# A transformer-style block on one core: first tile in halves, gain row by matmuls, sinks and mask steps later, last product by column halves

## The chip, the cores and the metric

The kernel runs on one core of a Trainium2 chip. Its time is the device time of one execution in microseconds (us); the figure for a kernel is the median of its runs. The names of the engines are those of the profile: PE is TensorE (matmuls and transposes; PEld are its weight loads), DVE is VectorE, ACT is ScalarE, POOL is GpSimd, SP is SyncE, which here only starts transfers.

## The reference, cut to what matters

The block works on 1024 tokens of 1024 channels. `rmsnorm` divides by the root of the mean square and multiplies by a gain per channel.

```python
h = rmsnorm(x, norm_g)                                 # per token: x * rsqrt(mean(x*x) + 1e-6) * norm_g
q, k, v, za, u, vs, zs, gm = split(h @ w_in)           # one combined projection
a = window_sink_attention(rope(q), rope(k), v, sinks)  # 16 heads, 2 key heads, window of chunks, a sink per head
a = (a * silu(za)) @ w_att_out
vs = layernorm(gelu(vs), sg_ln_g, sg_ln_b)
w = where(chunk-causal mask, sg_w, 0)                  # 8 groups of 128x128, over positions of a block of 128
sgo = ((gelu(u) * (w @ vs + sg_b)) * silu(zs)) @ w_sg_out
ga, gs = split(sigmoid(gm + b_merge))
x = x + (ga * a + gs * sgo) @ w_o
out = rmsnorm(x, final_g)
```

## The kernel before

**Tiles and number format.** Tokens and channels are cut into eight tiles of 128. The weights lie packed as 82 tiles of 128x1024 in DRAM. Every product is made of three matmuls on operands that are split into a high part (a cast, on ACT, L154) and a low part (what the cast left out, on DVE, L155): high by high, high by low, low by high. Most projections go through `gemm_pair`, which makes a 2x2 block of products with seven products instead of eight, from sums of the weight tiles and sums of the activations (`b11`, `t1`, `t2`, `b21`, `t3`, `b22`, `t4`). `product` (matmuls of L364) issues one of the seven: four slices of the contraction by three matmuls, 12 in all, each 128x128 by 128x512.

**Order of the work.** A scheduler orders most stages on each engine from the data dependences and the order of the source, so the order in the source is not that of an engine's queue; `after(a, b)` puts instruction a behind b. The attention stage has an order of its own, written out. Transfers are started by the queue of SP, some by POOL's and a few by ACT's; they leave a queue in the order in which it holds them.

**The start.** Thirteen matmuls without use for the result (`keep_busy`, L543) run on PE while the first data come. SP's queue starts the load of token tile 0 (512 KB), the broadcast of the row `norm_g` to all 128 partitions (4 KB read for each partition, 512 KB written), two weight tiles of the vs projection, token tile 1, and so on. For each token tile `scale_of` squares and sums a row on ACT (L571), `rstd_of` turns the sum into the factor in six steps (L132 on DVE, the root on ACT at L134, then four on DVE, the last at L144: a reciprocal and one Newton step), and `normed_tile` scales by the factor and the gain row on DVE in two halves (L585), transposes on PE (L591), casts the high part on ACT (L594), takes the low part on DVE (L595) and keeps a plain copy on ACT. `split_vs` splits the weight tiles; the low part of the first one is POOL's work (L621), that of the others DVE's. `vs_gemm(t)` makes, for one token tile, half of the vs channels: eight slices by three matmuls (L605) into one accumulator. The second half follows for all eight token tiles at once in eight accumulators.

**The two steps that move.** The sinks (16 numbers, spread over 128 partitions) are loaded on SP's queue with the last loads of this stage, and DVE turns their sign (L736, `nsink_sb`); the result is used in the attention stage. The mixing weights of the gating stage are loaded behind them, and DVE sets the masked quarter of each to zero (L757). They are used in the gating stage, which makes four calls of `gemm_pair`; in each, a DVE addition at L406 is the last to set `term[0]`.

**The end.** Four pairs of token tiles go through the last projection in the order of `T_ORDER`. In the last pair (p = 3) four products remain at the end: `by_b22`, `by_t3`, `by_b21`, and then `t4`, which completes the first half of the channels of row 1 (the second token tile of the pair). `add_and_square` adds the residual to a product (DVE, L1715) and squares and sums it on ACT (L1717). The factor for row 0 and row 1 comes from `rstd_of` with the first half's sum as its base. `scale_and_store` scales by factor and gain on DVE (L1737), or, where POOL has multiplied by the gain ahead of time (`scaled`), by the factor alone on ACT, and stores four pieces of 128x512, three started by SP and the last by ACT (L1735):

```python
        product(acc, ready[n, 6], ob["t4"], False)
        add_and_square(1, 0, acc, 1.0)
        scale_and_store(0)
        scale_and_store(1)
```

## Time and profile before

| | us |
|---|---|
| median of 3 runs | 929.79 (929.11, 929.79, 932.47) |
| profiled execution | 928.11 |
| span of its trace | 926.3 (granted clock 0.999 of full) |

By stretch of the span (busy us):

| stretch | what runs | PE | DVE | ACT | POOL |
|---|---|---|---|---|---|
| 0 to 30 | first tiles, first vs products | 23.96 | 19.03 | 20.67 | 3.24 |
| 30 to 160 | vs, its gelu, start of gating | 129.87 | 90.40 | 64.23 | 23.60 |
| 160 to 300 | gating, queries and keys | 140.00 | 95.06 | 57.63 | 27.88 |
| 300 to 560 | attention among others | 258.33 | 204.59 | 192.51 | 43.55 |
| 560 to 760 | branch outputs | 197.61 | 146.47 | 108.59 | 21.56 |
| 760 to 905 | branch outputs, last projection | 143.68 | 123.15 | 80.43 | 16.22 |
| 905 to 926 | last products, norm, stores | 13.93 | 12.98 | 6.75 | 5.06 |

The profile is of one execution, whose own time stands in the first table. A row of the instructions in order of time reads: start in us from the span's start, duration, engine, line of the kernel and operation, output<-inputs by the program's names, shapes, and in brackets how long the engine stood idle just before and what released it. A row of a stretch reads: stretch, its length, busy time and number of instructions of each engine, granted TensorE clock (1.00 is full), mean busy share of the 16 DMA engines, and GB/s. Busy times of PE are of matmuls that overlap in a pipeline, and their ends are modelled.

### The profile page before, as it was taken

The numbers are of one execution on the slowest core, as the hardware profiler recorded it, in microseconds if no ns is written. First come the engines' busy times: TensorE is split into PE (matmuls) and PEld (weight loads), VectorE is DVE, ScalarE is ACT, GpSimd is POOL, SyncE is SP. The second block draws the span as 40 slices with busy tenths as digits, with TensorE's granted clock in tenths as the row PEclk, the third lists the DMA queues.
The fourth block names the chain that finished last, engine by engine and source line by source line (L and its number), as shares of the span: only waits on it lengthen the run. The fifth ranks groups of instructions, "written<-read, shape, count | busy, mean of one in ns | idle before, by whom it ended". The sixth has DMA issues, their size and how long they took to land.

```text
span 926.3 us, 13136 instructions
## 1 busy us (share of the span) xinstructions
PE 907.4 (98%) x4285; PEld 749.9 (81%) x4285; DVE 691.7 (75%) x1234; ACT 530.8 (57%) x1054; POOL 141.1 (15%) x209
## 2 busy tenths in 40 slices
PE   7999999999999999999999999999999999999996
PEld 5788888888888888888888887888887887888885
DVE  6784776556678767777887778766598789579996
ACT  6973433334444556877778777434475475467443
POOL 1002222213011001321211110011100111210012
PEclk9999999999999999999999999999999999999999
DMA  7237788877778989999999994775568564998633
GB/s 261 92 114 218 178 146 185 175 189 219 239 267 259 283 266 308 203 266 271 260 343 246 241 269 138 278 257 187 174 207 319 176 205 151 297 314 286 206 112 116
DMA packets 128588, 206.62 MB, mean 223 GB/s; under 512 B 12584, under 2 KB 59176, under 8 KB 128520
## 3 DMA queue, kind: packets, MB, share of 16 engines
q1 hardware_dynamic: 107000, 146.79, 50.0%
q0 software_dynamic: 21376, 58.73, 26.3%
q8 instruction: 34, 0.56, 0.3%
q14 instruction: 34, 0.28, 0.1%
q10 hardware_dynamic: 144, 0.26, 0.1%
HBM read 148.98 MB, written 90.31 MB: 258 GB/s over the span
## 4 chain that ended last, share of the span: by engine, by line
PE 34%; DVE 14%; ACT 7%; issue 4%; DMA 3%; SPq 0%; ACTq 0%; DVEq 0%
PE ps_mm L364 17%; PE ps_o L364 10%; PE ps_tp L364 2%; ACT pr L1171 2%; PE ps_sc L364 2%; DVE sm L1161 2%; DVE pTb L1243 1%; DVE aT L1274 1%; ACT pr L1194 1%; DVE wl L155 1%; DVE bq L184 1%; PE ps_o L1260 1%; PE ps_sc L1136 1%; ACT aT L1273 1%; DMA s<-sums 1%
## 5 line engine op out<-in xcount | busy, mean ns | idle before, releaser
L154 ACT CAST wh<-s 128x1024 fp32r<-128x1024 f32 (+1 forms) x78 | 78.0, 1002 | 81.7 <-PE ps_mm L364 39.8
L155 DVE TENSOR_TENSOR wl<-s,wh 128x1024 fp32r<-128x1024 f32 (+1 forms) x78 | 91.6, 1174 | 20.9 <-ACT wh L154 20.7
L155 DVE TENSOR_TENSOR wl<-wr,wh 128x1024 fp32r<-128x1024 f32 (+1 forms) x64 | 60.3, 945 | 56.7 <-ACT wh L154 56.2
L154 ACT CAST wh<-wr 128x1024 fp32r<-128x1024 f32 (+1 forms) x64 | 53.0, 829 | 77.6 <-PE ps_mm L364 37.7
L310 POOL DMA_DIRECT2D sums<-in_w_dram x48 | 37.2, 936 | 212.3 <-PE ps_mm L605 63.2
L1171 ACT ACTIVATE pr<-ps_sc,sm 128x192 f32<-128x192 f32 (+2 forms) x128 | 51.2, 407 | 30.6 <-DVE sm L1162 22.0
L364 PE MATMUL ps_o<-T_b22h,wh 128*128 128x512 f32 x148 | 59.4, 401 | 0.0
L364 PE MATMUL ps_o<-T_t1h,wh 128*128 128x512 f32 x148 | 58.6, 396 | 0.3 <-ACT wh L154 0.2
L364 PE MATMUL ps_o<-T_t1h,wl 128*128 128x512 f32 x148 | 57.8, 391 | 0.2 <-DVE wl L155 0.2
L364 PE MATMUL ps_o<-T_b22l,wh 128*128 128x512 f32 x148 | 57.8, 391 | 0.0
L364 PE MATMUL ps_o<-T_b22h,wl 128*128 128x512 f32 x148 | 57.8, 390 | 0.0
L364 PE MATMUL ps_o<-T_t1l,wh 128*128 128x512 f32 x148 | 57.7, 390 | 0.0
L364 PE MATMUL ps_mm<-T_b11h,wl 128*128 128x512 f32 x140 | 54.8, 392 | 2.0 <-DVE wl L155 2.0
L364 PE MATMUL ps_mm<-T_t2h,wh 128*128 128x512 f32 x140 | 55.5, 396 | 0.0
L364 PE MATMUL ps_mm<-T_t4h,wh 128*128 128x512 f32 x140 | 55.0, 393 | 0.3 <-DVE x L402 0.3
L364 PE MATMUL ps_mm<-T_b11h,wh 128*128 128x512 f32 x140 | 55.1, 394 | 0.0
L364 PE MATMUL ps_mm<-T_t3h,wh 128*128 128x512 f32 x140 | 54.8, 391 | 0.0
L364 PE MATMUL ps_mm<-T_b11l,wh 128*128 128x512 f32 x140 | 54.7, 391 | 0.0
L364 PE MATMUL ps_mm<-T_t3h,wl 128*128 128x512 f32 x140 | 54.6, 390 | 0.0
L364 PE MATMUL ps_mm<-T_t4h,wl 128*128 128x512 f32 x140 | 54.6, 390 | 0.0
L364 PE MATMUL ps_mm<-T_t2h,wl 128*128 128x512 f32 x140 | 54.6, 390 | 0.0
L364 PE MATMUL ps_mm<-T_t4l,wh 128*128 128x512 f32 x140 | 54.5, 390 | 0.0
(370 smaller groups left out, 2469.0 us busy)
## 6 DMA issues: line engine op xcount, KB each, us to landing
wr<-in_w_dram SPq DMA_DIRECT2D x80, 256.0 KB
sums<-in_w_dram POOLq DMA_DIRECT2D x24, 512.0 KB, 6.5
s<-sums SPq DMA_DIRECT2D x24, 512.0 KB
wr<-in_w_dram SPq DMA_DIRECT2D x16, 512.0 KB
q_hl<-qhl SPq DMA_DIRECT2D x16, 512.0 KB
q<-q_hl SPq DMA_DIRECT2D x64, 128.0 KB
y_dr<-x POOLq DMA_DIRECT2D x28, 256.0 KB, 6.6
sums<-in_w_dram POOLq DMA_DIRECT2D x24, 256.0 KB, 7.9
```

Source lines behind the costliest of these rows:

```text
L154: nc.scalar.copy(hi, src)
L155: return nc.vector.tensor_sub(lo, src, hi.bitcast(F32))
L184: op(dst[:, i : i + 2, :], a[:, i : i + 2, :], c[:, i : i + 2, :])
L310: return lambda: paced(nc.gpsimd.dma_start(dst, src, accum_op=op))
L364: nc.tensor.matmul(acc, lt, rt, start=fresh and k == 0 and n == 0, stop=k == 3 and n == 2, skip_group_check=True,)
L1136: nc.tensor.matmul(sc[:, i, lo:hi], q_of[:, c, i * P : (i + 1) * P], kt[:, f, lo:hi], start=f == 0, stop=f == 1,)
L1161: nc.vector.tensor_reduce(st.nmax[:, c, :], st.sc[c][:, :, lo:hi], axis=mybir.AxisListType.X, op=ALU.min)
L1171: nc.scalar.activation(st.pr[:, i, place_of(c, lo, hi)], st.sc[c][:, i, lo:hi], AF.Exp, bias=st.nmax[:, c, i : i + 1], scale=-1.0, accum_o ...
L1194: nc.scalar.mul(v, v, st.inv[:, c, i : i + 1])
L1243: nc.vector.tensor_sub(st.b[lo, cols(c)], st.ends[hi, 0:256], st.b[hi, cols(c)].bitcast(F32))
L1260: nc.tensor.matmul(st.po[:, cs], lt, rt, start=i == 0, stop=i == len(terms) - 1, skip_group_check=True)
L1273: nc.scalar.copy(dst, out_of(there))
```

## The change

Start: the load of token tile 0 is two transfers of 256 KB. The gain row is loaded once (4 KB, started by ACT's queue) and spread to the partitions by two matmuls with a row of ones, one for each half, into two PSUM banks, from which `normed_tile` reads it. Four dummy matmuls stand ahead of them and one behind, in another bank, instead of 13. `rstd_of` adds the base within ACT's root and folds the last multiplication into the step before; the eight-column case has a function of its own with the old steps. The square of token tile 0 is taken in two halves, the first half's sum becoming the base of the factor. The first weight tile is split in two halves, on ACT and POOL. In `vs_gemm(0)` the first two slices are ordered by part: two high by high, two high by low, two low by high. The sign of the sinks is turned behind the last addition of the gating stage; the zeroing of the mixing weights stands behind the last low part of x. The transfers of both keep their place on SP's queue.

End: the last product is made in two halves of 256 columns of 12 matmuls each (`last_by_halves`), each followed by its own addition and square; the first half's sum becomes the base of the factor. Row 1's remaining pieces are scaled and stored in quarters: two on DVE, started by SP, two on ACT, started by ACT. Row 0's two stores are both started by SP.

```diff
@@ -97,6 +97,8 @@
+    g_row = mtile([P, D], F32, "wh", 3)[0:1, :]
+    nc.scalar.dma_start(g_row, norm_g.unsqueeze(0))
     plain = mtile([P, D], F32, "wl", 3)[:, 0:HALF]
@@ -126,20 +128,29 @@
-    def rstd_of(ss, scale, base=EPS, n=1):
-        ve = mtile([P, n], F32, f"st{n}", 16 if n == 1 else 5)
-        nc.vector.tensor_scalar(ve[:], ss, scale, base, op0=ALU.mult, op1=ALU.add)
-        rt = mtile([P, n], F32, f"st{n}", 16 if n == 1 else 5)
+    def stat():
+        return mtile([P, 1], F32, "st1", 16)
+    def rstd_of(ss, scale, base=None):
+        rt, r0, v, r = (stat() for _ in range(4))
+        nc.scalar.activation(rt[:], ss, AF.Sqrt, bias=eps_sb[:] if base is None else base[0], scale=scale)
+        nc.vector.tensor_scalar(
+            v[:], ss, -0.5 * scale, -0.5 * EPS if base is None else base[1], op0=ALU.mult, op1=ALU.add
+        )
+        nc.vector.reciprocal(r0[:], rt[:])
+        nc.vector.scalar_tensor_tensor(v[:], v[:], r0[:], r0[:], op0=ALU.mult, op1=ALU.mult)
+        nc.vector.tensor_scalar(r[:], v[:], 1.5, r0[:], op0=ALU.add, op1=ALU.mult)
+        return r
+    def rstd_of_tiles(var):
+        ve, rt, r0, e = (mtile([P, NT], F32, f"st{NT}", 5) for _ in range(4))
+        nc.vector.tensor_scalar(ve[:], var, 1.0, EPS, op0=ALU.mult, op1=ALU.add)
         nc.scalar.activation(rt[:], ve[:], AF.Sqrt)
-        r0 = mtile([P, n], F32, f"st{n}", 16 if n == 1 else 5)
         nc.vector.reciprocal(r0[:], rt[:])
-        e = mtile([P, n], F32, f"st{n}", 16 if n == 1 else 5)
-        if n == 1:
-            nc.vector.scalar_tensor_tensor(e[:], ve[:], r0[:], r0[:], op0=ALU.mult, op1=ALU.mult)
-        else:
-            nc.vector.tensor_mul(e[:], ve[:], r0[:])
-            nc.vector.tensor_mul(e[:], e[:], r0[:])
+        nc.vector.tensor_mul(e[:], ve[:], r0[:])
+        nc.vector.tensor_mul(e[:], e[:], r0[:])
         nc.vector.tensor_scalar(e[:], e[:], -0.5, 1.5, op0=ALU.mult, op1=ALU.add)
@@ -351,9 +362,9 @@
-    def product(acc, part, form, fresh, middle=lambda: None):
+    def product(acc, part, form, fresh, middle=lambda: None, cols=slice(0, HALF)):
         wh, wl = part
-        bh, bl = form
+        bh, bl = (v[:, :, cols] for v in form)
         for k in range(4):
@@ -525,15 +536,15 @@
-    def load_x(t):
+    def load_x(t, parts=1):
         xt = raw_tile()
-        nc.sync.dma_start(xt[:], x[t * P : (t + 1) * P, :])
+        for c in range(parts):
+            cs = slice(c * D // parts, (c + 1) * D // parts)
+            nc.sync.dma_start(xt[:, cs], x[t * P : (t + 1) * P, cs])
         return xt
-    x_in = {0: load_x(0)}
-    g_in = mtile([P, D], F32, "wh", 3)
+    x_in = {0: load_x(0, 2)}
     junk = mtile([P, D], F32, "wl", 3)
-    nc.sync.dma_start(g_in[:], norm_g.partition_broadcast(P))
@@ -542,8 +553,12 @@
-    idle = bank("sc")
-    keep_busy(13)
+    idle = bank("o")
+    keep_busy(4)
+    g_in = [bank("sc") for _ in range(2)]
+    for j in range(2):
+        nc.tensor.matmul(g_in[j][:], plain[0:1, 0:P], g_row[:, half_of(j)], start=True, stop=True)
+    keep_busy(1)
@@ -563,11 +578,18 @@
-    casts = []
+    casts, los = [], []
         xt = x_in[t] if t in x_in else load_x(t)
-        ss = mtile([P, 1], F32, "st1", 16)
+        if t == 0:
+            s0, s1, base, half_base = (stat() for _ in range(4))
+            for c, ss in enumerate((s0, s1)):
+                nc.scalar.activation(junk[:, half_of(c)], xt[:, half_of(c)], AF.Square, accum_out=ss[:])
+            nc.vector.tensor_scalar(base[:], s0[:], 1.0 / D, EPS, op0=ALU.mult, op1=ALU.add)
+            nc.vector.tensor_scalar_mul(half_base[:], base[:], -0.5)
+            return xt, rstd_of(s1[:], 1.0 / D, (base[:], half_base[:]))
+        ss = stat()
         square = nc.scalar.activation(junk[:], xt[:], AF.Square, accum_out=ss[:])
@@ -583,7 +605,7 @@
             nc.vector.scalar_tensor_tensor(
-                xt[:, cs], xt[:, cs], r[:], g_in[:, cs], op0=ALU.mult, op1=ALU.mult
+                xt[:, cs], xt[:, cs], r[:], g_in[j][:], op0=ALU.mult, op1=ALU.mult
             )
@@ -592,7 +614,7 @@
             casts.append(nc.scalar.copy(hi, p3))
-            nc.vector.tensor_sub(lo, p3, hi.bitcast(F32))
+            los.append(nc.vector.tensor_sub(lo, p3, hi.bitcast(F32)))
             turned.append((f[f"f{j + 1}{t // 4 + 1}"][:, :, tokens(t)], p3))
@@ -617,13 +639,23 @@
         else:
-            nc.scalar.copy(hi, raw)
-            nc.gpsimd.tensor_tensor(lo, raw, hi.bitcast(F32), op=ALU.subtract)
+            for k in range(2):
+                nc.scalar.copy(hi[:, k, :], raw[:, k, :])
+                nc.gpsimd.tensor_tensor(lo[:, k, :], raw[:, k, :], hi[:, k, :].bitcast(F32), op=ALU.subtract)
         vs_w.extend((hi[:, k, :], lo[:, k, :]) for k in range(2))
         acc = bank("mm")
-        for k in range(KC):
+        if t == 0:
+            by_part = [[], [], []]
+            for k in range(2):
+                hi, lo = (v[:, k, :] for v in quarter_of(t, 0))
+                wh, wl = vs_w[k]
+                for part, pair in zip(by_part, ((hi, wh), (hi, wl), (lo, wh))):
+                    part.append(pair)
+            for n, (lt, rt) in enumerate(by_part[0] + by_part[1] + by_part[2]):
+                nc.tensor.matmul(acc[:], lt, rt, start=n == 0, stop=False)
+        for k in range(2 if t == 0 else 0, KC):
             vs_step(acc[:], t, k, *vs_w[k])
@@ -733,7 +765,6 @@
         )
-    nc.vector.tensor_scalar_mul(nsink_sb[:], sink_sb[:], -1.0)
     nc.sync.dma_start(bm_sb[:], b_merge)
@@ -754,7 +785,7 @@
     nc.sync.dma_start(mix_w[:], sg_w)
-    nc.vector.memset(mix_w[64:128, :, 0:64], 0.0)
+    after(nc.vector.memset(mix_w[64:128, :, 0:64], 0.0), los[-1])
     ones = mtile([P, P], F32, "ones", 1, pool)
@@ -763,7 +794,7 @@
     def normalize():
-        r = rstd_of(mv[:, :, 1], 1.0, n=NT)
+        r = rstd_of_tiles(mv[:, :, 1])
         for t in range(NT):
@@ -832,6 +863,7 @@
     stage.close()
+    after(nc.vector.tensor_scalar_mul(nsink_sb[:], sink_sb[:], -1.0), term[0])
@@ -1713,16 +1745,46 @@
             pace[0] = (nc.vector.tensor_sub if sign < 0 else nc.vector.tensor_add)(z, z, src)
-            ss = mtile([P, 1], F32, "st1", 16)
+            ss = stat()
             nc.scalar.activation(bank("tp")[:], z, AF.Square, accum_out=ss[:])
             if i in sq:
-                sq[i] = rstd_of(ss[:], 1.0 / D, sq[i][:])
+                sq[i] = rstd_of(ss[:], 1.0 / D, sq[i])
             else:
-                nc.vector.tensor_scalar(ss[:], ss[:], 1.0 / D, EPS, op0=ALU.mult, op1=ALU.add)
-                sq[i] = ss
+                sq[i] = based(ss, EPS)
+        def based(ss, base):
+            b, minus = stat(), stat()
+            nc.vector.tensor_scalar(b[:], ss[:], 1.0 / D, base, op0=ALU.mult, op1=ALU.add)
+            nc.vector.tensor_scalar_mul(minus[:], b[:], -0.5)
+            return b[:], minus[:]
+        def last_by_halves():
+            for c in range(2):
+                cs = slice(c * 256, (c + 1) * 256)
+                z = xr[:, 2, cs]
+                product(acc[:, cs], ready[n, 6], ob["t4"], False, cols=cs)
+                pace[0] = nc.vector.tensor_add(z, z, acc[:, cs])
+                ss = stat()
+                nc.scalar.activation(bank("tp")[:, cs], z, AF.Square, accum_out=ss[:])
+                if c == 0:
+                    sq[1] = based(ss, sq[1][0])
+                else:
+                    sq[1] = rstd_of(ss[:], 1.0 / D, sq[1])
+            r = sq[1]
+            row = slice((t + 1) * P, (t + 2) * P)
+            v = scaled[1, 1][:]
+            for c in range(2):
+                cs = slice(c * 256, (c + 1) * 256)
+                z = xr[:, 2, cs]
+                nc.vector.scalar_tensor_tensor(z, z, r[:], g_out[:, 0, cs], op0=ALU.mult, op1=ALU.mult)
+                nc.scalar.mul(v[:, cs], v[:, cs], r[:])
+                nc.sync.dma_start(out[row, cs], z)
+                nc.scalar.dma_start(out[row, HALF + c * 256 : HALF + (c + 1) * 256], v[:, cs])
@@ -1732,7 +1794,7 @@
                     nc.scalar.mul(v, v, r[:])
-                    (nc.scalar if i else nc.sync).dma_start(out[row, half_of(e)], v)
+                    nc.sync.dma_start(out[row, half_of(e)], v)
                     continue
@@ -1787,10 +1849,8 @@
         by_b21()
-        product(acc, ready[n, 6], ob["t4"], False)
-        add_and_square(1, 0, acc, 1.0)
         scale_and_store(0)
-        scale_and_store(1)
+        last_by_halves()
     stage.close()
```

## The prediction

> **What bounds the kernel now.** I read the page's first part, then the busy times by stretch, then the instructions in order of time for the first 25 us and the last 11 us: by the order of instructions these are the only places where the change moves anything on an engine, one 128x8 step apart.
>
> ```profile
> span 926.3 us, 13136 instructions
> PE 907.4 (98%) x4285; PEld 749.9 (81%) x4285; DVE 691.7 (75%) x1234; ACT 530.8 (57%) x1054; POOL 141.1 (15%) x209
> ```
> ```profile
> 2.00:10.00 8.00, 6.80 (x22) 1.00 0.95 356
> ...
> 20.00:30.00 10.00, 8.45 (x45) 1.00 0.38 132
> ...
> 40.00:50.00 10.00, 10.00 (x50) 1.00 0.32 106
> ```
>
> The columns of the second fence are stretch, length, PE busy, granted clock, DMA share, GB/s. PE is busy 98% of the span, and a stretch such as 40 to 50 has no gap. So what PE's start and its end save is kept as long as PE stays the bound between them, and only the gaps before 30 us (1.2 in 2 to 10, 1.55 in 20 to 30, more between) and the work behind PE's last product can give anything. The start, in order of time:
>
> ```profile
> 1.92 5.11 PE L543 MATMUL ps_sc<-T_b22l 128*128 128x512 f32 x13 [1.92 <-DVE T_b22l L539]
> ...
> 4.64 1.06 ACT L571 ACTIVATE wl<-wr 128x1024 f32<-128x1024 f32 x1 [2.41 <-DMA wr<-in_x_dram]
> ...
> 5.82 0.15 DVE L132 TENSOR_SCALAR st<-st 128x1 f32<-128x1 f32 x1 [3.96 <-ACT wl L571]
> 6.01 0.20 ACT L134 ACTIVATE st<-st 128x1 f32<-128x1 f32 x1 [0.22 <-DVE st L132]
> ...
> 6.89 0.16 DVE L144 TENSOR_TENSOR st<-st,st 128x1 f32<-128x1 f32 x1
> 7.08 1.41 DVE L585 SCALAR_TENSOR_TENSOR wr<-wr,st,wh 128x512 f32<-128x512 f32 x2
> 7.74 1.05 ACT L620 CAST T_t1h<-T_t3h 128x1024 fp32r<-128x1024 f32 x1 [1.53 <-DMA T_t3h<-in_w_dram]
> ...
> 8.70 0.58 ACT L594 CAST T_b11h<-ps_tp 128x512 fp32r<-128x512 f32 x1
> 8.87 2.36 POOL L621 TENSOR_TENSOR T_t1l<-T_t3h,T_t1h 128x1024 fp32r<-128x1024 f32 x1 [7.43 <-ACT T_t1h L620]
> ...
> 9.31 0.69 DVE L595 TENSOR_TENSOR T_b11l<-ps_tp,T_b11h 128x512 fp32r<-128x512 f32 x1 [0.81 <-ACT T_b11h L594]
> ...
> 9.33 0.50 PE L605 MATMUL ps_mm<-T_t1h,T_b11h 128*128 128x512 f32 x1
> ...
> 10.67 1.06 ACT L571 ACTIVATE wl<-wr 128x1024 f32<-128x1024 f32 x1
> 10.80 1.52 DVE L155 TENSOR_TENSOR T_t1l<-T_t3h,T_t1h 128x1024 fp32r<-128x1024 f32 x1 [0.21 <-ACT T_t1h L154]
> ...
> 11.29 0.50 PE L605 MATMUL ps_mm<-T_t1l,T_b11h 128*128 128x512 f32 x1 [1.46 <-POOL T_t1l L621]
> ...
> 12.99 2.00 ACT L154 CAST T_t2h<-T_t4h 128x1024 fp32r<-128x1024 f32 x2
> ...
> 14.09 0.50 PE L605 MATMUL ps_mm<-T_t2h,T_b21h 128*128 128x512 f32 x1
> ...
> 20.86 0.39 PE L605 MATMUL ps_mm<-T_t1h,T_b11l 128*128 128x512 f32 x1
> 21.42 0.17 DVE L736 TENSOR_SCALAR nsink_sb<-sink_sb 128x8 f32<-128x8 f32 x1 [1.70 <-DMA sink_sb<-in_sinks_dram]
> ...
> 22.70 0.63 PE L591 MATMUL ps_tp<-ident,wr 128*128 128x128 f32 x4 [1.45 <-DMA wT<-in_sg_w_dram]
> ```
>
> Three things end last in turn: POOL's low part of the weights (PE waits until 11.29), ACT's queue (T_t2h, PE waits until 14.09), and the sinks, which DVE awaits until 21.42 with the end of tile 2's factor queued behind them (PE waits until 22.70; the row names wT, but it was DVE that came late). The end:
>
> ```profile
> 916.05 0.39 PE L364 MATMUL ps_mm<-T_t4h,wh 128*128 128x512 f32 x1
> ...
> 917.03 0.60 ACT L1717 ACTIVATE ps_tp<-bq 128x512 f32<-128x512 f32 x1 [1.28 <-DVE bq L1715]
> ...
> 918.54 0.39 PE L364 MATMUL ps_mm<-T_t4h,wl 128*128 128x512 f32 x1
> ...
> 919.59 0.75 DVE L1737 SCALAR_TENSOR_TENSOR bq<-bq,st,bq 128x512 f32<-128x512 f32 x1
> 919.79 0.58 ACT L1717 ACTIVATE ps_tp<-bq 128x512 f32<-128x512 f32 x1
> ...
> 922.60 0.40 ACTq L1735 DMA_DIRECT2D out_dram<-g  x1
> ```
>
> The last 12 products start in 916.05 to 918.54; a chain of sum, square, factor and scaling follows until the stores leave at 922.60.
>
> **The change part by part: the start.** All times are on the clock of before.
>
> The factor of tile 0. The second half of x lands when the whole tile did, 4.64: as many bytes lie ahead of it. Its square is half as wide (0.58 at 919.79, against 1.06: -0.48); the root follows on ACT at once, without L132's step (6.01-5.82 = -0.19); the last product is folded in (7.08-6.89 = -0.19). Scaling starts at 7.08-0.86 = 6.22.
>
> The weights. SP's queue carries x, the broadcast g and the weights in this order:
>
> ```profile
> 2.00:3.50 1.50, 1.50 (x4) 1.00 0.89 339
> 3.50:5.50 2.00, 2.00 (x7) 1.00 0.87 252
> 5.50:14.00 8.50, 6.01 (x26) 1.00 1.02 412
> ```
>
> 339 GB/s for 1.5 us are the 0.52 MB of x; the next 2.0 us at 252 GB/s are the 0.52 MB of g, slower than what follows. With one row in its place the first weight tile lands 2.0 us earlier, 5.74 instead of 7.74 (bounds: at the rate of its neighbours g would be 0.52/412 = 1.3 us; nothing, if the landing hangs on something else). The next one is 1.27 behind, 7.01.
>
> ACT is then the chain. Two half casts (8.70-7.74 = 0.96): 6.70. The second weight tile's cast, which now stands ahead of the first cast of x: 7.01+1.0 = 8.0. The cast of x could start 1.62 after the scaling (8.70-7.08), at 7.84, so it starts at 8.0, and the first product 0.63 later (9.33-8.70), at 8.65: 0.7 earlier. POOL's halves start behind the first half cast, 6.3+2.36 = 8.65: that wait is gone. What is late next: DVE has the second tile's low part (8.1+1.52) ahead of the low part of x (0.69), so the products with it start at 10.4. The four products put ahead of them, 0.226 each, are over at 9.55: a new wait of 0.8; the last eight end at 12.2. ACT meanwhile: two casts of x until 9.1, then square, copy, root, copy (12.99-10.67 = 2.32) until 11.4, T_t2h (1.0) until 12.45. The product of 14.09 starts at 12.55: **lead 1.55**; PE waits 0.35 for it, ACT is the last.
>
> Tile 1 repeats the rows of before with this lead: 20.86 becomes 19.3. Tile 2's scaling, at 21.7 (L144 and two hops behind the sinks' step), loses DVE's 1.70 of idle time as well: 18.4. Its transposes came 1.0 behind it (22.70) and come at 19.4, about when PE does. So of 22.70-20.86-0.226 = 1.61 **1.5** go. The sinks' step moves behind the gating stage's last L406 and the zeroing behind the last low part of x, both beside dense PE work; their loads have long landed, and the DMA issues stay where they were in SP's order. Of the gaps left after 22.70 (20 to 30 is 8.45 busy, and starts held back by ACT's and DVE's queues count on top) I take **0.7**, bounds 0 and 1.2: ACT's order has two table loads fewer, and no zeroing stands between factors on DVE.
>
> The gain row by matmuls is off the path:
>
> ```profile
> L778 PE MATMUL ps_sc<-wT,ones x4: 590/590/591, 121.9 to 157.9; 128*128 128x512 f32 x4
> ```
>
> Five dummies end at about 4, two such matmuls follow, at twice 0.59 if PE is slow so early, done by 6.2, when the scaling starts. Their reader on DVE now reads PSUM, as L595 does; bounds 0 and 0.1.
>
> **The end.**
>
> ```profile
> 486.57 0.41 PE L1260 MATMUL ps_o<-pTb,v 128*128 128x256 f32 x2
> ```
> ```profile
> L1243 DVE TENSOR_TENSOR pTb<-ps_tp,pTb 64x256 fp32r<-64x256 f32 x60 | 25.3, 421 | 1.3
> ...
> L1260 PE MATMUL ps_o<-pTb,v 128*128 128x256 f32 x60 | 12.9, 291 | 0.0
> ```
>
> The pitch of the wide products is (918.54-916.05)/11 = 0.226, that of 256 columns 0.41-0.29 = 0.12. The first half is complete at 916.05+11x0.12+0.29 = 917.7, its sum (0.42) at 918.15. In DVE's order there follow row 0's four small steps (0.9, until 919.05), its scaling (0.75, 919.8) and two steps of the new base (0.4, 920.2), and only then the second half's sum. PE may start the second half only when the first sum is read (918.15) and is ready at 919.85, so DVE's queue ends last, and this sum comes at 920.2 instead of 919.0. From there the chain is shorter: sum 0.42, half a square 0.5, root to factor 0.9 (6.01 to 6.89), quarter scaling 0.42. Stores leave SP at 922.55 and 923.0, ACT at 923.0 and 923.4, instead of both at 922.60. The last piece has a quarter of the 0.52 MB: 0.8+0.13/356 GB/s = 1.2 after the first issue, less than the 1.5 of the whole. **I take 0** for the end, bounds -0.5 and +0.8.
>
> **Sum.** -(1.55+1.5+0.7)+0 = -3.75. The profiled execution took 928.11 (926.3 and 1.8 around it), 1.68 under the median of 929.79 of the runs; I subtract from the median: 926.0.
>
> **A rule against the change.** 13 dummies in 5.11 us are 0.39 apart, the later products 0.226, though the granted clock reads 1.00 for both. The Trainium skill, "TensorE: Matmul & The Clock Gate" (Part 1 and Part 4), has PE at half rate until matmuls have filled a free-running window of about 3.4 us, and does not count transposes as work. By it, seven matmuls in place of 13 can leave the first products slow, and the sum is -2.9 (third rival); by the row, whose pace has changed before 7.03, it is -3.75.
>
> **The rivals.** Two need rows of the attention stage, where DMA is saturated:
>
> ```profile
> 400.00:420.00 20.00, 19.98 (x109) 1.00 1.06 244
> ```
> ```profile
> 400.33 6.99 DMA s<-sums
> ...
> 408.04 5.62 DMA q<-q_hl
> ```
>
> - Faster still: the weights' 2.0 come through whole because ACT's order is not what ends last, all later gaps close (1.2), the end gains 0.3: -5.0, 924.8. For it: the new waits of 0.8 and 0.35 rest on DVE's 1.52, which the rows show once. Chance 0.27.
> - The weights land no earlier: ACT's chain from 7.74 on stays, lead 0 at 14.09, -1.5-0.7 = -2.2, 927.6. Against it: the stretch at 252 GB/s. Chance 0.10.
> - PE keeps the 0.39 pitch through the first dozen products: 12x0.17 = 2.0, of which the waits of 0.8 and 0.35 hide 1.15: -2.9, 926.9. Chance 0.08.
> - The change doesn't carry: the lead is used up in the saturated stage, 929.8. Against it: PE is busy 19.98 of 20 there. Chance 0.04.
> - Slower: PE comes 4 us early to loads of that stage that do not. The two waits above are on the chain but covered by PE's work; if both lie open once, 12.6-3.75 = +8.9, 938.7. It decides where these moves keep their old time; against it: they are paced by PE's own results and shift with it. Chance 0.05.
>
> **How the numbers follow.** The forecast has 0.46, its own range -2.9 to -4.9. A change counts from 0.5% (4.65 us) on, about what a measurement of this kernel can tell. Faster by that: the first rival and 0.06 of the forecast, 0.33. Slower: 0.05. Between: 0.62. The range leaves out the last two rivals and the tips of the others: 924.8 less 0.9, 927.6 plus 1.2, as the three runs shown are up to 2.7 off their median: 923.9 to 928.8.
>
> **What would show it.** Right: the first product of tile 0 near 8.65, the one with T_t2h near 12.55, no gap before tile 2's transposes, an equal lead at 100 and at 900 us; in the end the second half's sum behind row 0's scaling on DVE, the stores at 922.5 to 923.4 less the lead. Wrong: the first weight cast still at 7.7; a gap of PE beyond 30 us that was not there; a lead that shrinks between 300 and 560 us; a pace of 0.39 beyond 10 us.

## The result, and the profile after

| | before | after |
|---|---|---|
| median of 7 runs, us | 931.03 (929.11 to 932.47) | 927.66 (926.00 to 928.71) |
| ratio | | 0.9968 [0.9954, 0.9981] |
| profiled execution, us | 928.11 | 928.34 |
| its span, us, and granted clock | 926.3, 0.999 | 926.6, 0.996 |

The changed kernel is 3.4 us faster by the medians, which is within the 0.5% that counted as no change; 926.0 had been predicted. The two profiled executions differ by 0.2 us the other way. So the traces have to say not only what was gained but where a gain of the start can get lost. One thing in the table matters for that: the profiled execution of before is 2.9 under the median of its kernel, that of after 0.7 over the median of its own, and their granted clocks differ. The page of after, its first part (span; busy time, share and instructions):

```profile
span 926.6 us, 13154 instructions
...
PE 910.7 (98%) x4293; PEld 751.9 (81%) x4293; DVE 692.0 (75%) x1232; ACT 531.0 (57%) x1058; POOL 142.3 (15%) x210
```

PE is busy 3.3 us longer than before on almost the same matmuls. By stretch (length; busy time and instructions of PE, PEld, DVE, ACT and POOL; granted clock, DMA share, GB/s):

```profile
2.00:10.00 8.00, 8.00 (x17) 4.00 (x17) 3.05 (x9) 5.17 (x11) 2.07 (x2) 1.00 0.95 341
20.00:30.00 10.00, 9.99 (x55) 7.92 (x54) 8.35 (x22) 9.32 (x20) 0.00 (x0) 1.00 0.51 177
```

Both stretches that had gaps, 2 to 10 and 20 to 30, are now full. Full is not fast, though, as the instructions in order of time show:

```profile
4.34 3.78 PE L560 MATMUL ps_sc<-wh,wl 1*128 1x512 f32 x4
...
6.46 0.75 DVE L607 SCALAR_TENSOR_TENSOR wr<-wr,st,ps_sc 128x512 f32<-128x512 f32 x1 [0.27 <-PE ps_sc L560]
...
7.23 1.14 ACT L643 CAST T_t1h<-T_t3h 128x512 fp32r<-128x512 f32 x2 [1.75 <-DMA T_t3h<-in_w_dram]
...
7.93 2.51 POOL L644 TENSOR_TENSOR T_t1l<-T_t3h,T_t1h 128x512 fp32r<-128x512 f32 x2 [6.49 <-ACT T_t1h L643]
...
8.05 2.03 PE L613 MATMUL ps_tp<-ident,wr 128*128 128x128 f32 x8
...
9.56 1.96 DVE L166 TENSOR_TENSOR T_t1l<-T_t3h,T_t1h 128x1024 fp32r<-128x1024 f32 x1 [0.65 <-ACT T_t1h L165]
...
10.06 1.22 PE L657 MATMUL ps_mm<-T_t1h,T_b11h 128*128 128x512 f32 x2
...
10.48 1.42 SPq L765 DMA_DIRECT2D sink_sb<-in_sinks_dram  x2
...
12.17 0.73 PE L657 MATMUL ps_mm<-T_t1h,T_b11l 128*128 128x512 f32 x2
...
14.40 0.50 PE L627 MATMUL ps_mm<-T_t2h,T_b21h 128*128 128x512 f32 x1
...
20.47 0.60 PE L613 MATMUL ps_tp<-ident,wr 128*128 128x128 f32 x4
```

The gain row's matmuls (two of them in the source, four in the trace, each of 1.06, 3.78 in all) end at 8.12, the eight transposes follow at 8.05 and take 2.03 (1.27 before), and the first products have a pitch of 0.51, the next ones 0.23. The weights' first cast is at 7.23 (7.74 before). The first product starts at 10.06, 0.73 later than before, and the one with T_t2h at 14.40, 0.31 later. Only then the lead appears: the transposes of tile 2 start at 20.47 (22.70 before). Both loads of the sinks are now issued at 10.48; before, the second left only at 16.12.

At 98 us the same DVE instruction stands in both traces (first before, then after), 2.01 apart:

```profile
98.74 1.23 DVE L155 TENSOR_TENSOR wl<-s,wh 128x1024 fp32r<-128x1024 f32 x1 [2.51 <-ACT wh L154]
```
```profile
96.73 1.23 DVE L166 TENSOR_TENSOR wl<-s,wh 128x1024 fp32r<-128x1024 f32 x1 [2.51 <-ACT wh L165]
```

This lead stays within 0.15 at the DVE rows compared up to 320 us. Then attention begins, and here the two traces part. Before:

```profile
335.60 1.35 DVE L1094 TENSOR_TENSOR x<-x,rot 128x512 f32<-128x512 f32 x2 [3.37 <-DMA rot<-s_dr]
...
342.50 1.39 PE L1136 MATMUL ps_sc<-k,q 128*128 128x64 f32 x8 [0.49 <-ACT pr L1171]
```

After:

```profile
334.86 1.37 DVE L1126 TENSOR_TENSOR x<-x,rot 128x512 f32<-128x512 f32 x2 [4.63 <-DMA rot<-s_dr]
...
338.95 1.28 ACT L1136 ACT_TABLE_LOAD   x1
...
341.79 1.39 PE L1168 MATMUL ps_sc<-k,q 128*128 128x64 f32 x8 [1.78 <-ACT pr L1203]
```

The load of the gate rows (rot) releases DVE at 335.60 and at 334.86: of the 2.0 us the load came only 0.74 earlier, though the first of its four transfers was issued 1.84 earlier (327.19, 329.03 before). DVE's multiplication by these rows stands ahead of the addition (L417) for which ACT's silu waits, then the load of the Exp table (338.95), then the first exponentials (341.04), and PE's second group of scores waits for those. It stood idle 0.49 before and 1.78 now. Behind this gap the granted clock falls (the figure behind the five engines' counts):

```profile
343.00:344.00 1.00, 1.00 (x5) 0.81 (x5) 0.96 (x5) 0.96 (x3) 0.00 (x0) 0.57 0.98 320
344.00:345.00 1.00, 1.00 (x4) 0.81 (x3) 0.44 (x3) 0.80 (x5) 0.51 (x1) 0.50 0.99 381
345.00:346.00 1.00, 1.00 (x5) 0.58 (x5) 0.00 (x0) 0.00 (x0) 0.88 (x2) 0.50 1.14 318
```

It is 0.57, 0.50 and 0.50, then 0.72, and 1.00 in the trace of before: about 3.4 us at half clock, which cost 1.7. At 410.85, on the clock of before, after is 0.91 late: 1.3 us went into the gap and 1.6 into the clock behind it. Some 0.6 comes back near 723 us, where PE before waited 0.29 for an addition, and in the end it is 0.16 behind at 914.25. The end itself:

```profile
916.06 0.28 PE L375 MATMUL ps_mm<-T_t4h,wh 128*128 128x256 f32 x1
...
918.16 0.39 PE L375 MATMUL ps_mm<-T_t4h,wh 128*128 128x256 f32 x1 [0.51 <-DVE bq L1771]
...
918.84 0.75 DVE L1799 SCALAR_TENSOR_TENSOR bq<-bq,st,bq 128x512 f32<-128x512 f32 x1
...
919.89 0.42 DVE L1771 TENSOR_TENSOR bq<-bq,ps_mm 128x256 f32<-128x256 f32 x1
...
922.43 0.81 SPq L1786 DMA_DIRECT2D out_dram<-bq  x2
...
922.45 0.85 ACTq L1787 DMA_DIRECT2D out_dram<-g  x2
```

From the first matmul of the last product to the end of the span are 10.54 us (10.25 before).

### The profile page after: what moved, and what is told of

It is laid out like the page before. It is cut to its first block, busy times and chain, and to the rows that moved or that the text cites. A ratio compares the mean times of both kernels' runs of the same rounds, so it can differ in the third digit from the quotient of the medians.

```text
span 926.6 us, 13154 instructions
## 1 busy us (share of the span) xinstructions
PE 910.7 (98%) x4293; PEld 751.9 (81%) x4293; DVE 692.0 (75%) x1232; ACT 531.0 (57%) x1058; POOL 142.3 (15%) x210
## 4 chain that ended last, share of the span: by engine, by line
PE 43%; DVE 11%; ACT 6%; issue 3%; DMA 1%; ACTq 0%; DVEq 0%
PE ps_mm L375 21%; PE ps_o L375 12%; PE ps_tp L375 3%; PE ps_sc L375 2%; ACT pr L1203 2%; PE ps_sc L1168 2%; PE ps_o L1292 1%; DVE sm L1193 1%; ACT pr L1226 1%; DVE pTb L1275 1%; DVE bq L195 1%; DVE wl L166 1%; DVE aT L1306 1%; DMA vi<-v_dr 1%; ACT aT L1305 1%
## 5 line engine op out<-in xcount | busy, mean ns | idle before, releaser
L375 PE MATMUL ps_mm<-T_t4h,wh 128*128 128x512 f32 (+1 forms) x144 | 55.7, 387 | 0.5 <-DVE bq L1771 0.5
L375 PE MATMUL ps_mm<-T_t4h,wl 128*128 128x512 f32 (+1 forms) x144 | 55.3, 384 | 0.0
L375 PE MATMUL ps_mm<-T_t4l,wh 128*128 128x512 f32 (+1 forms) x144 | 55.2, 383 | 0.0
```

What stands on the lines that cost most here:

```text
L375: nc.tensor.matmul(acc, lt, rt, start=fresh and k == 0 and n == 0, stop=k == 3 and n == 2, skip_group_check=True,)
```

## The experiments

Every one is given with its time, the time of before on the same chip, and places of its trace. A ratio is of medians, with its 95% interval; runs with (1) are single executions. "Weights' cast" is the start of the first cast of the first weight tile; "product" is the start of the first product and of the one with T_t2h; "lead" is how much earlier than in the profiled before the same DVE instruction starts, at 98.74 and 410.85 us of before; "gap" is PE's idle time ahead of the second scores; "clock" is the granted clock in the ten microseconds around it (340 to 350); "tail" runs from the last product's first matmul to the end of the span.

| | median us (runs) | before | ratio | weights' cast | product | lead 99 | gap | clock | lead 411 | tail |
|---|---|---|---|---|---|---|---|---|---|---|
| before | | | | 7.74 | 9.33, 14.09 | 0 | 0.49 | 1.00 | 0 | 10.25 |
| after | 927.66 (7) | 931.03 | 0.9968 [0.9954, 0.9981] | 7.23 | 10.06, 14.40 | 2.01 | 1.78 | 0.83 | -0.91 | 10.54 |
| e1 | 927.69 (12) | 930.68 | 0.9962 [0.9942, 0.9981] | 7.70 | 9.29, 14.05 | 1.67 | 0.74 | 1.00 | 1.48 | 10.23 |
| e2 | 928.97 (12) | 930.68 | 0.9982 [0.9966, 0.9998] | 7.14 | 10.01, 14.35 | 1.99 | 1.77 | 0.83 | -0.83 | 10.57 |
| e4 | 926.21 (10) | 930.68 | 0.9955 [0.9938, 0.9973] | 7.52 | 10.40, 15.18 | 1.07 | 0.22 | 1.00 | 1.42 | 10.54 |
| e5 | 927.98 (12) | 930.68 | 0.9970 [0.9952, 0.9988] | 7.82 | 10.69, 15.91 | 0.51 | filled | 1.00 | -0.23 | 10.48 |
| e6 | 928.15 (10) | 929.67 | 0.9983 [0.9966, 0.9999] | 7.36 | 10.22, 14.53 | 1.65 | 0.97 | 1.00 | 1.21 | 10.53 |
| e7 | 927.27 (1) | 929.67 | | 6.01, half | 10.99, 15.61 | 0.85 | 1.18 | 1.00 | 0.17 | 10.51 |
| e8 | 927.79 (10) | 929.67 | 0.9975 [0.9960, 0.9990] | 7.84 | 9.52, 14.09 | 2.29 | 1.66 | 0.83 | -0.79 | 10.55 |
| e9 | 925.49 (1) | 929.67 | | 7.06 | 10.09, 14.23 | 2.20 | 0.89 | 1.00 | 1.85 | 10.39 |
| e10 | 926.39 (1) | 930.05 | | 6.44 | 9.09, 13.96 | 2.44 | filled | 1.00 | 1.67 | 10.54 |
| e11 | 930.00 (1) | 930.05 | | 7.81 | 9.39, 14.16 | 1.69 | 2.00 | 0.83 | -2.19 | 10.23 |
| e12 | 925.76 (12) | 930.05 | 0.9960 [0.9941, 0.9979] | 7.61 | 10.63, 15.74 | 0.75 | filled | 1.00 | 0.83 | 10.11 |
| e13, after again | 928.07 (12) | 930.05 | 0.9982 [0.9967, 0.9997] | 5.71 | 9.90, 14.01 | 2.41 | 0.43 | 1.00 | 2.54 | 10.53 |

Three questions are asked: what gave the lead of 2.0, what takes it away at 340 us, and what the new start and the new end are worth by themselves.

**What gave the lead: the sinks.** e1 is before with the two steps moved and nothing else; e2 is after with both steps back in their old places.

```diff
 e1 (on before)
-    nc.vector.tensor_scalar_mul(nsink_sb[:], sink_sb[:], -1.0)
...
-    nc.vector.memset(mix_w[64:128, :, 0:64], 0.0)
+    after(nc.vector.memset(mix_w[64:128, :, 0:64], 0.0), los[-1])
...
     stage.close()
+    after(nc.vector.tensor_scalar_mul(nsink_sb[:], sink_sb[:], -1.0), term[0])
```

> The kernel before, with only the sinks' step and the zeroing moved behind the work of their stages. The lead is how much earlier the same DVE row starts than in the trace of before. Theory A (these moves carry the gain, and the rest of the new start costs 0.3): nothing changes until 20 us, DVE's wait of 1.70 is gone, the lead at 60 to 320 us is 1.6 to 2.3. Theory B (half of the lead of 2.0 comes from the new start): 0.8 to 1.2. By both the lead is cut in the 340s, where DVE waits for the gate rows, so that the whole comes out between -3 and +1 us.

> The kernel after, with the sinks' step and the zeroing back in their old places. Theory A: the product with T_t2h still starts near 14.4, the wait for the sinks is back, and the lead at 60 to 320 us is -0.5 to 0.3. Theory B: it is 0.8 to 1.2. The whole: within 1.5 us of before by A, about 1 us faster by B.

e1 alone brings a lead of 1.67, although its start is that of before (9.29, 14.05), and by its median as much as the whole change. That speaks for the step's place. But e2, with the step in its old place, keeps the lead (1.99), because there is no wait any more:

```profile
18.49 0.15 DVE L768 TENSOR_SCALAR nsink_sb<-sink_sb 128x8 f32<-128x8 f32 x1
```

The step runs without a wait at 18.49, where before it waited 1.70 until 21.42. What differs in e2 from before is SP's queue: the sinks' second load is no longer behind the load of a token tile that waits for a free buffer. (The broadcast of g is gone from that queue; whether this alone brought the new order was not tried.) e11 tests the place in the queue: it is before, with the step in its place, and only the two loads put earlier in the queue.

```diff
 e11 (on before)
     x_in[2] = load_x(2)
+    of_head = sinks.rearrange("(c e r) -> e c r", e=2, r=2)
+    for e in range(2):
+        nc.sync.dma_start(
+            sink_sb[e * 64 : (e + 1) * 64].rearrange("p (c r) -> p c r", r=2), of_head[e].partition_broadcast(64)
+        )
```

> The kernel before, with the two loads of the sinks issued together in SP's queue, ahead of the load of the fourth token tile, which waits for a free buffer; the step on DVE stays about where it was. In before the second of these loads stood behind that token tile and was issued at 16.12, in after both were issued at 10.48. Theory K (the old wait was this place in the queue, and after removes it twice, by the order of the loads and by moving the step): both loads are issued near 10, the wait of 1.70 is gone, the lead at 60 to 320 us is 1.4 to 2.0, as with the step moved (1.67). Rival L (the step itself has to move): the wait stays, lead -0.3 to 0.3.

```profile
4.76 2.37 SPq L646 DMA_DIRECT2D sink_sb<-in_sinks_dram  x2
...
18.42 0.16 DVE L736 TENSOR_SCALAR nsink_sb<-sink_sb 128x8 f32<-128x8 f32 x1
...
343.03 1.39 PE L1136 MATMUL ps_sc<-k,q 128*128 128x64 f32 x8 [2.00 <-ACT pr L1171]
```

Both loads are issued from 4.76 on, earlier than expected, the step runs at 18.42 without a wait, and the lead is 1.69, that of e1. So the wait is removed twice in this change, and either edit does it. The one execution of e11 also shows that a lead can be lost whole: its gap at 343 us is 2.00, the clock falls there as in after, and at 410.85 it is 2.19 late.

**What takes the lead away: the entry to attention.** In e4 the gate multiplications of the second pair stand behind the last addition, so that ACT no longer waits for the load through them. In e5 the gap is filled with eight matmuls without use for the result.

```diff
 e4 (on after)
-            if hooked[0] >= 4:
+            if hooked[0] >= (6 if m else 4):
...
-                    nc.vector.tensor_mul(q[:], q[:], gates.pop(0))
+                    by_gate = nc.vector.tensor_mul(q[:], q[:], gates.pop(0))
+                    if m:
+                        after(by_gate, term[0])
 e5 (on after)
+            if p == 0:
+                spare = bank("tp")
+                row = hb["t1"][0][:, 0, :]
+                for _ in range(8):
+                    nc.tensor.matmul(spare[:], row[:, 0:P], row, start=True, stop=True)
             of(scores, b)
```

> The kernel after, with the multiplications by the gate rows of the second zs pair put behind the pair's last addition on DVE, so that the addition, the silu on ACT and the exponential's table no longer stand behind a load. Theory C (the lead of 2.0 dies at the entry to attention because DVE waits for these rows, and PE's idle time of 1.8 there makes the clock fall to half for about 3 us): PE's gap near 340 shrinks to below 0.7, the clock stays at 1.00 between 342 and 348, the lead stays at 1.0 to 2.0 through the attention stage, and the kernel is 2 to 3 us faster than the profiled run of after. Rival D (the loads of the attention stage itself, the keys and queries, come last): the gap stays at 1.8 with another releaser, time as after.

> The kernel after, with eight matmuls without use (0.23 each) ahead of the second scores of the attention stage, where PE was idle for 1.8 us. Theory C: the idle time is as long, but the clock no longer falls, so the 1.6 us by which the lead fell at half clock come back: lead near 0.5 in the attention stage, where after has -0.9, and about 1.5 us faster than after. Rival E (the clock falls for another reason, such as power or the DMA load): the clock still falls to 0.5, and the time is as after or 0.5 us more.

```profile
341.09 1.39 PE L1170 MATMUL ps_sc<-k,q 128*128 128x64 f32 x8 [0.22 <-ACT pr L1205]
```

In e4 the gap is 0.22, the clock stays at 1.00, and the lead is larger behind the entry (1.42) than ahead of it (1.07). The lead was small here, and with a like one e7 kept its full clock at a gap of 1.18; so it is the gap that this trace shows closed, and the medians have to show what that is worth. Against before on the same chip e4 is 4.5 us faster; against e5 it is 1.8, but those two intervals overlap. In e5 the clock stays full too, but the dummies themselves take time (lead 0.51 to -0.23), and by the rows of its exponentials the gap would have been only about 1.3: it does not decide. e10 repeats it with a larger lead, on the start of e8.

> The reordered start with wide gain matmuls (lead 2.3 at 60 us, then a gap of 1.66 at the entry to attention, the clock at 0.5 for 3 us and a lead of -0.7), with the eight matmuls without use in that gap. The gaps so far: 1.66, 1.77 and 1.78 were followed by the half clock, 0.22, 0.49, 0.74, 0.89 and 1.18 were not. Theory C: no half clock with the gap filled, lead in the attention stage 1.2 to 1.8. Rival E (the arrival ahead of time itself, or the load on DMA, brings the half clock): the clock falls to 0.5 in the 340s all the same, lead -1 to 0.

The clock stays full again and 1.67 of 2.44 us remain; the gap would have been some 1.3, so it does not decide either. The table does it as far as it goes: gaps of 1.66, 1.77, 1.78 and 2.00 were followed by half clock, gaps of 0.22 to 1.18 in seven traces were not. Other places of the traces narrow it: 1.45 in before (ahead of 22.70) and 1.28 in e6 (ahead of 415.23) were not followed by it either. Rival E, that coming early brings the fall, does not sort the traces: e9, e13 and e10 came 2.20 to 2.44 early without one, e11 and e2 1.69 and 1.99 early with one. That the DMA load has no part in it is not shown.

e13 is the changed kernel without an edit, to see whether the entry always costs this.

> The kernel after once more, for a comparison on the same chip: 926 to 929 us by its seven runs, with the lead at 60 us between 0.5 and 2.0 by when the first weights land, and the half clock in the 340s in the executions whose gap there is over about 1.5 us.

```profile
5.71 1.14 ACT L643 CAST T_t1h<-T_t3h 128x512 fp32r<-128x512 f32 x2 [0.36 <-DMA T_t3h<-in_w_dram]
...
8.06 2.03 PE L613 MATMUL ps_tp<-ident,wr 128*128 128x128 f32 x8
...
332.84 1.53 DVE L1126 TENSOR_TENSOR x<-x,rot 128x512 f32<-128x512 f32 x2 [3.12 <-DMA rot<-s_dr]
...
339.93 1.39 PE L1168 MATMUL ps_sc<-k,q 128*128 128x64 f32 x8 [0.43 <-ACT pr L1203]
```

It does not. In this execution the lead was 2.41, more than the 0.5 to 2.0 expected, and the gate rows released DVE at 332.84, 2.76 earlier than before; the gap is 0.43, and the span 923.1 instead of 926.6. So the same program either keeps its lead or loses 2.9 us of it, by when one load lands. The landings of the other runs with a lead of 1.6 or more are in line: 333.67 in e9, 334.04 in e1 and 334.31 in e6, which kept their lead here, 334.73 in e8, 334.83 in e2 and 335.31 and 336.77 in e11, which did not. Why one load of the same transfers lands 2 us sooner or later is open.

How often this happens can be read from the mean granted clock. The nine traces without a stretch at half clock inside the work have 0.998 or 0.999, the five with one (after, e2, e8 and e11 here, e6 further on) have 0.996 or 0.997. Taken as a sign of such a stretch, this sorts the executions without a trace too:

| | 0.998 or more: executions, median us | less: executions, median us |
|---|---|---|
| before, in the experiments | 12, 928.58 | 63, 930.75 |
| after and e13 | 8, 926.08 | 11, 928.71 |
| e4 | 9, 926.15 | 1, 929.71 |

So before loses clock more often than after, and its profiled execution, at 0.999, is one of its few without a loss; that of after, at 0.996, has one. Like with like, after is 2.0 to 2.5 us faster: the size of the lead. Where the other executions of before lose their clock no trace shows; e11, which is before but for two loads, lost it at this entry. e4 has only one execution of ten below 0.998, which fits an entry that no longer opens the gap.

**The start by itself.** e6 replaces the one-row gain matmuls by matmuls over all 128 rows (the row set to zero but for its first partition) and holds the first weight cast behind the root of tile 0's factor. e8 also puts the second weight tile's cast and low part behind those of x. e7 loads the first weight tile as two transfers.

```diff
 e6 (on after)
-    g_row = mtile([P, D], F32, "wh", 3)[0:1, :]
+    g_row = mtile([P, D], F32, "wh", 3)
+    nc.gpsimd.memset(g_row[:], 0.0)
...
-        nc.tensor.matmul(g_in[j][:], plain[0:1, 0:P], g_row[:, half_of(j)], start=True, stop=True)
+        nc.tensor.matmul(g_in[j][:], plain[:, 0:P], g_row[:, half_of(j)], start=True, stop=True)
...
-                nc.scalar.copy(hi[:, k, :], raw[:, k, :])
+                after(nc.scalar.copy(hi[:, k, :], raw[:, k, :]), roots[0])
 e8 (on e6)
+            if c == 1:
+                after(nc.scalar.copy(hi, raw), casts[1])
+                after(nc.vector.tensor_sub(lo, raw, hi.bitcast(F32)), los[1])
 e7 (on after)
-        nc.sync.dma_start(vs_raw[c // 2][:, c % 2, :], w[W_VS + c])
+        for k in range(1 if c else 2):
+            ks = slice(0, D) if c else half_of(k)
+            nc.sync.dma_start(vs_raw[c // 2][:, c % 2, ks], w[W_VS + c][:, ks])
```

> The kernel after, with the gain row spread by matmuls over 128 rows of which 127 are zero, in place of one row (the zeroing is on POOL, ahead of the row's load; the first weight cast is held behind the root, as in after). In after two products start 0.51 apart until about 12.2, although PE had been busy since 1.9; where the weights land at 7.5 or 7.8 in place of 7.2 this slow pace costs 1 to 1.5 us of lead. Theory F (matmuls over one row do not bring PE to its full pace, wide ones do): the eight transposes take 1.3 us in place of 2.03, the first products stand 0.23 to 0.35 apart, the gain matmuls end before 7.5, and the lead at 60 to 320 us is 2.0 to 2.4 whenever the weights land. Rival G (matmuls of this number type, or too few of them, are the cause): transposes and products as slow as in after.

> As the wide gain matmuls, and on ACT the cast of the second weight tile behind the two first casts of x, on DVE its low part behind the two low parts of x, as in the kernel before. If the orders on ACT and DVE were what cost the new start its lead at the first product (10.06 against 9.33) and at the one with T_t2h (14.40 against 14.09), the first product starts at 9.0 to 9.4 and that with T_t2h at 13.5 to 13.9, and the lead at 60 us is 2.3 to 2.9. If the weights' landing is what matters, nothing changes beside the wide one (within 0.3).

> The kernel after, with the first weight tile loaded in two halves of 256 KB. The first cast of the weights started at 7.23 in after, 1.5 us later than its bytes stand in the running sum of what the DMA engines moved. If the queue lets the transfers behind it share the bandwidth (theory J), or if some of the engines are behind the others, the first half lands well before the second: the first half cast starts at 5.9 to 6.6, the second near 7.2. If the landing hangs on a fixed start-up of the weights' load (rival K), both start as in after, 7.1 to 7.8.

```profile
4.66 2.67 PE L563 MATMUL ps_sc<-wh,wl 128*128 128x512 f32 x4
...
7.40 1.43 PE L616 MATMUL ps_tp<-ident,wr 128*128 128x128 f32 x8
...
10.22 0.74 PE L660 MATMUL ps_mm<-T_t1h,T_b11h 128*128 128x512 f32 x2 [1.39 <-ACT T_b11h L619]
...
425.69 1.79 PE L1171 MATMUL ps_sc<-k,q 128*128 128x192 f32 x8 [3.11 <-DMA q<-q_hl]
```

The wide matmuls are over in 2.67 instead of 3.78, the transposes take 1.43 instead of 2.03 and the first pair of products 0.74 instead of 1.22: with them PE has its pace at 7.4, with one-row matmuls not before 12.2. It brings nothing by itself: the first product is at 10.22, since it waits 1.39 for the cast of x, and the lead is 1.65 where 2.0 to 2.4 were expected. Far behind the start, e6 shows another loss:

```profile
425.00:430.00 5.00, 4.31 (x20) 4.12 (x21) 0.00 (x0) 0.17 (x1) 0.00 (x0) 0.66 0.75 237
```

Scores at 425.69 waited 3.11 for the load of q, and in the stretch from 425 to 430 the granted clock is 0.66; the lead of 1.21 at 411 us is -4.47 at 828. e8 has the same start but for two instructions:

```profile
8.54 2.51 POOL L651 TENSOR_TENSOR T_t1l<-T_t3h,T_t1h 128x512 fp32r<-128x512 f32 x2 [5.93 <-ACT T_t1h L650]
...
9.52 0.73 PE L664 MATMUL ps_mm<-T_t1h,T_b11h 128*128 128x512 f32 x2 [0.61 <-ACT T_b11h L619]
...
10.93 1.22 DVE L645 TENSOR_TENSOR T_t1l<-T_t3h,T_t1h 128x1024 fp32r<-128x1024 f32 x1
```

Its first product is at 9.52, 1.68 behind the weights' cast at 7.84; in e6, with the same gain matmuls and the cast order of after, it is 2.86 behind (7.36 to 10.22). So that order costs about 1.2 us at the first product when the weights are late. All the same 9.52, 14.09 and the lead of 2.29 each fall just short of what was expected, and the lead is lost at the entry (gap 1.66). In e7 the first half was cast at 6.01, but the cast went ahead of tile 0's root on ACT, so that the scaling began only at 8.34 and the product at 10.99; whether a smaller transfer lands earlier is not settled by one run.

What the slow pace of PE costs when the weights come late shows in e5, where they were cast at 7.82:

```profile
10.69 1.22 PE L657 MATMUL ps_mm<-T_t1h,T_b11h 128*128 128x512 f32 x2 [0.60 <-ACT T_b11h L616]
...
13.78 0.63 PE L627 MATMUL ps_mm<-T_t1h,T_b11h 128*128 128x512 f32 x1
```

The pairs take 1.22, and single products still 0.63 at 13.78, against 0.39 at 12.74 in after. The two runs with the one-row matmuls and late weights, e4 (7.52) and e5, have leads of 1.07 and 0.51 instead of 2.0.

**The end by itself.** e9 makes both halves of the product first and scales row 0 behind both additions.

```diff
 e9 (on after)
                 product(acc[:, cs], ready[n, 6], ob["t4"], False, cols=cs)
+            for c in range(2):
+                cs = slice(c * 256, (c + 1) * 256)
+                z = xr[:, 2, cs]
...
+            scale_and_store(0)
             r = sq[1]
...
-        scale_and_store(0)
         last_by_halves()
```

> The kernel after, with both halves of the last product issued before the first half is added, and row 0's scaling on DVE behind the second half's addition. From the first matmul of the last product to the end of the span it took 10.25 us before, 10.54 after. Theory H (PE's wait of 0.5 for the first addition, and row 0's steps ahead of the second addition, took the gain of the halves): the second addition comes 0.6 earlier, the last stores 0.5 to 0.9 earlier, the stretch is 9.6 to 10.0. Rival I (the last stores' own time from issue to landing sets the end): 10.4 to 10.6.

```profile
913.31 0.28 PE L375 MATMUL ps_mm<-T_t4h,wh 128*128 128x256 f32 x1
...
916.38 0.75 DVE L1773 TENSOR_TENSOR bq<-bq,ps_mm 128x256 f32<-128x256 f32 x2 [0.33 <-PE ps_mm L375]
...
917.05 0.74 DVE L1802 SCALAR_TENSOR_TENSOR bq<-bq,st,bq 128x512 f32<-128x512 f32 x1
...
918.01 0.29 ACT L137 ACTIVATE st<-st,st 128x1 f32<-128x1 f32 x1 [0.27 <-DVE st L1761]
...
919.58 0.86 ACTq L1790 DMA_DIRECT2D out_dram<-g  x2
```

PE has no wait left, but both additions now run only behind all 24 matmuls (916.38, 3.07 behind the first one), and row 0's scaling (917.05) is drawn between the second addition and the factor. The tail is 10.39: 0.15 better than after's, 0.14 worse than before's. Theory H had 9.6 to 10.0, rival I 10.4 to 10.6; it is at the edge of the rival's range.

**Put together.** e12 has the start of e8, the gates of e4 with four dummies, and the old end.

> After with the parts that the runs so far favour: wide gain matmuls and the old orders of ACT and DVE in the start (lead 2.3 at 60 us), the gate multiplications behind the last addition, four matmuls without use ahead of the second scores (0.9 us of the gap), and the end of the kernel before (10.25 us from the last product to the end of the span, in place of 10.54). If these add up: no half clock in the 340s, lead 1.8 to 2.6 through the attention stage, 2.5 to 4.5 us faster than after and 5.5 to 7.5 faster than before. If the attention stage's loads take the lead: as after.

```profile
1.72 0.52 ACTq L102 DMA_DIRECT2D wh<-in_norm_g_dram  x1
...
5.27 3.75 PE L563 MATMUL ps_sc<-wh,wl 128*128 128x512 f32 x4 [0.75 <-DMA wh<-in_norm_g_dram]
...
8.82 2.16 PE L616 MATMUL ps_tp<-ident,wr 128*128 128x128 f32 x8
```

It is at 925.76, faster than before (0.9960 [0.9941, 0.9979]), but by 4.3 and not the 5.5 to 7.5 expected, and 2.3 under the 928.07 of after on the same chip, where those two intervals overlap. Its start fell short (lead 0.75), and the lines show why: the zeroing of the gain row on POOL holds its load back to 1.72 (0.73 in after), the row came late, PE stood idle 0.75, and then even the wide matmuls took 3.75 and the transposes 2.16, as slow as in after. In e6, e8 and e10 the row's load was issued at 1.72 too, but PE waited at most 0.51 for it and the matmuls took 2.57 to 2.67. So wide matmuls alone do not bring the pace; in e12 they did not. The tail is 10.11, with the old products and stores and the new factor: 0.14 under before, so that it is the halves, not the factor, that cost after its 0.29. e4, with one edit, does as well: 926.21 on its chip.

## Why the prediction was right or wrong

The median came out 1.7 over the forecast, inside its range, and the measured -3.4 is near the sum of -3.75. But terms of the sum were wrong and made up for each other. The start is the second rival's: the weights came at most a little earlier, and 927.66 is its 927.6.

- **The weights.** Step: without the broadcast of g the first tile lands 2.0 earlier, 5.74. Over ten executions with the new order the cast starts at 5.71 to 7.84, in after at 7.23. The bound "nothing, if the landing hangs on something else" was nearer than the value, and of the lead of 1.55 at the product with T_t2h there is nothing: it came 0.31 late. Why the landing varies stays open.
- **ACT's chain.** From the cast to the first product 2.91 were worked out. With late weights that was right: 2.83 in after, 2.87 to 2.88 in e2, e4 and e5. With weights at 5.71, in e13, it was 4.19, for another chain ended last (the gain matmuls, below). To the product with T_t2h 6.81 were worked out; it was 7.17 in after and 8.09 in e5.
- **DVE's low part.** Sized at 1.52 by the row of before, where 0.4 of it lay beside POOL's subtraction, it took 1.96 in after, with 0.9 beside it (9.56 to POOL's end at 10.44), and 1.22 in e8, with 0.1 (10.93 to 11.05).
- **The gain matmuls.** "Done by 6.2" failed: they ended at 8.12. The step took two rows of 0.59 each for two matmuls, but there are four rows, and of 1.06. Even with the weights at 5.71, in e13, the first product started at 9.90, not 8.65: the transposes came at 8.06, behind them. "Off the path" holds only as long as the weights are late.
- **PE's pace.** The third rival was real. The Trainium skill ("TensorE: Matmul & The Clock Gate", Part 1 and Part 4) starts PE at half rate and does not count transposes as activity. The trace agrees in the pairs of 1.22. The runs add that matmuls over one row, four rows of 1.06, did not bring the pace either, while those over 128 rows did in e6, e8 and e10, and not in e12, where PE had stood idle for 0.75. In the stretch 2 to 10 the granted clock reads 1.00 throughout, so this pace has to be read from durations. In after the waits hid it, as the rival had it; in e4 and e5 it lay open.
- **The sinks.** Size right (1.5 worked out; the leads of e1 and e11 are 1.67 and 1.69), cause half right: "the DMA issues stay where they were in SP's order" failed, and the new order alone removes the wait (e2, e11).
- **The lead.** So the start gave 2.01 instead of 3.75: 1.67 from the sinks, -0.31 at the product with T_t2h, and 0.65 that is left over. That is near the 0.7 taken for "gaps left after 22.70", but no row measures it by itself, and its place was wrong: ACT copies the finished accumulators 0.29 later at 19 us (19.30 against 19.01), 0.77 earlier at 34 (33.68 against 34.45) and 1.72 earlier at 42 (40.37 against 42.09), so that much of the lead shows only behind 30 us, where the prediction saw no gap.
- **Keeping it.** "What PE's start saves is kept as long as PE stays the bound" failed in the profiled execution at 335 us, at a wait on a load that was in the trace of before, with PE idle for 0.49 and thus easily missed. A lead moves PE against a load that may move less, and the gap it opens costs twice, once itself (1.3) and once in the clock behind it (1.6). The prediction had no term for the clock at all, and the trace that it read is one of the few of before without such a loss. The slower rival had this mechanism in the wrong place, and there it was seen once: e6's wait for q, whose lead went from 1.21 to -4.47. The Trainium skill ("TensorE: Matmul & The Clock Gate", table of "Why this matters for your kernels") names idle gaps over about 3 us as the danger. The one of 3.11 in e6 agrees; at the entry 1.66 was enough, and the measurement decides.
- **The end.** Taken at 0 with bounds -0.5 and +0.8, it is +0.29. Its inner steps were right: the second addition was placed at 920.2 behind row 0's scaling and came at 919.89, PE's wait for the first sum was there (0.51). What failed is "the last piece has a quarter": the second quarter's issue is at 922.88, and from the last issue to the end of the span are 3.7 us, as in before (922.60). In both traces the 0.52 MB of row 1 move between 923.25 and 925.00 (300 GB/s on average) and the span ends 1.3 to 1.6 later: a smaller last piece does not make the four land sooner than the two.
- **Why the total fits all the same.** The median of before over 7 runs is 931.03, not the 929.79 that was subtracted from, so the gain of 3.4 is partly a slower before; by e13 (928.07 against 930.05, 12 and 23 executions) it is 2.0. Like with like by the clock it is 2.0 to 2.5, the lead that the start gave; and before loses clock in more of its executions (63 of 75) than after (11 of 19), which adds to it. That this comes near -3.75, with the weights' 1.55 missing, is luck.

## What to carry to other kernels

A gain early in a kernel can be lost at the first wait on something that does not come earlier with it, so look at every entry to a later stage for idle time that is small now and ends with a load; a reordering there (e4) kept what the start had won. Price such a gap together with the clock that follows it. Before two traces are compared, compare their mean granted clocks with those of the other executions of each kernel: here one was of the lucky kind and the other not, and the pair alone would have said that the change gains nothing. And before a load is called "in its old place", read the issue rows of its queue: what was taken out ahead of it moves it, and may do the whole job of an edit that looks like the cause.
